# Seven joined parts in place of two fourth products in the first feed-forward stage of an encoder

## The chip, the core and the metric

The kernel runs on one core of a Trainium2 chip. A core has a matrix engine (TensorE, "PE" in the profile, with its weight loads on a row of their own, "PEld"), two engines for elementwise work (VectorE, "DVE", and ScalarE, "ACT"), GpSimd ("POOL"), which here issues the DMAs that add to what lies in the buffer, and SyncE ("SP"), which issues plain DMAs. All five run their own queues in order and wait for each other by semaphores. The metric is device time in microseconds (us) of one execution; lower is better.

## The reference

A two-layer encoder over 512 tokens of 1024 channels, float32. Each layer is a feed-forward stage (FFN), a mixer and a second FFN; so there are four FFNs, and the one that the change touches is the first of layer 0.

```python
D_MODEL, SEQ, DEPTH, D_FF = 1024, 512, 2, 2816
...
def swiglu(x, w_in, w_out):
    gu = x @ w_in
    g, u = jnp.split(gu, 2, axis=-1)
    return (jax.nn.silu(g) * u) @ w_out
...
for l in range(DEPTH):
    x = x + 0.5 * swiglu(rms_norm(x, ffn1_norm[l]), ffn1_w_in[l], ffn1_w_out[l])
    x = x + mixer(rms_norm(x, mix_norm[l]), ...)
    x = x + 0.5 * swiglu(rms_norm(x, ffn2_norm[l]), ffn2_w_in[l], ffn2_w_out[l])
return rms_norm(x, final_norm)
```

## The kernel before

**Precision.** Every float32 operand is split into a high part (rounded, type fp32r) and a low part (the rest). One product of two operands is three matmuls: high x high, low x high, high x low (`run`, L392 to L406).

**Weights.** They come from HBM in granules of 128 x 1024 (two contraction tiles of 128, 512 columns each), 512 KB apiece, into nine "raw" buffers (`ffn_raw`, L2024). For each granule ScalarE writes the high part `whi` (L205, L207) and VectorE the low part `wlo` (L212, L214); there are three buffers of each. The class `Stream` walks one list of items made in advance (`stage_items`), and the products take them in that order (`ws.next`). When an item's high part is made, the loads of the next eight items are issued (`fetch`, FETCH). An item may be a sum of two granules: either VectorE adds the second (`sum`, L200), or GpSimd issues a DMA that adds the second one into the first one's buffer (L166). `then` names a granule that is added by such a DMA after the low part has been made, so that the buffer serves a later item.

**Seven products for eight.** The up and gate projections are done by blocks of 512 columns of w_in. A block is a 2 x 2 matrix product (two halves of the contraction, gate and up columns; two halves of the tokens) and is computed by a Strassen-like scheme in seven products instead of eight. They are named 1 to 7 here, as in the code; each takes two granules and 24 matmuls of 128 x 512, and their results are joined on ScalarE and VectorE (`snap`, `less`, `gate`, `times`). There are five blocks, `jb` 0 to 4, after a first part of 256 + 256 columns that is done plainly into four banks `pcl` (L694 to L706). Block 0 is the *single block* (L984 to L1024); blocks 1 and 2, and 3 and 4, are *pairs* (`pair_block`, L899).

**Products joined over a pair.** The product 2 of both blocks of a pair has the same activations, and the weights of the two blocks stand for the two columns of another 2 x 2 product, this time within the contraction half. So the two products 2 are done together as seven inner products `b1` to `b7`, of one granule and 6 matmuls each (`inner`, L735), spread over the two blocks. In the three later FFNs the first pair's products 4 are done in the same manner, as `d1` to `d7`: `begin_deep` (L867) is a generator; its first step makes four sums of the activations on VectorE (`inner_parts`), splits them into `vh` and `vl` (`inner_split`) and does d1 into the bank rA; each further `next` does one more. Four are done in the single block (d1, d5, d6, d3), two in block 1 (d2, d7) and one in block 2 (d4). `kv` and `kw` keep their sums until the block adds them to `pa` (L957). In the first FFN the generator is an iterator over five numbers, so these steps do nothing, and products 4 are done in full in both blocks (L973).

**Items.** `INNER` (L37) says behind which product each inner part's item stands; the single block's items in the first FFN are 1, 2, 5, 6, 7, 3, 4 (ORDER_0), two granules each. Of a pair's parts, d1 takes one granule a, d5 the sum d of two granules (by a DMA), d6 d + a and d3 d + b (VectorE), d2 the granule b, d7 a sum c (by a DMA), d4 one granule. In the first FFN, b6 is d + a by VectorE; in the later ones b5's buffer gets a added by a DMA after b5, and b6 takes it as it is.

**The first FFN's single block.** Its work on VectorE and ScalarE is held in program order (`tc.manual_schedule`, L985) up to the roots of the row norms (`norm.roots`), since the input x arrives only then. `spread_root` (L767) then writes the 512 roots to HBM and reads them back spread over all partitions (`rd`, `rr`), on SyncE's queue, where the raw loads are issued too. `plain_out` (L773), which needs `rr`, comes in block 2 (L919). Elsewhere the engines' orders are the scheduler's, by program order and readiness.

Of the kernel before, what the change touches and what calls it, by code (L numbers as in the profile page):

```python
# [35 lines left out]
DEEP = 1  # L36
# [18 lines left out]
PAIRS = (1, 3)  # L55
# [49 lines left out]
def encoder_kernel(  # L105
# [120 lines left out]
    def stage_items():  # L226
        items, st = [], 0

        def add(*a, **k):
            items.append(Item(*a, stage=st, **k))  # L230

        made = {}

        def strassen(s, name, idx, sizes, order, dma=False):
            r = made.setdefault((s, name("a"), idx), {}) if dma and len(order) < 7 and order[0] > 2 else {}
            for q, q2 in () if r else (("a", ""), ("b", ""), ("c", "a"), ("d", "c")):
                r[q] = [
                    Raw((s, name(q), idx, g), n, *[(s, name(z), idx, g) for z in q2]) for g, n in enumerate(sizes)
                ]
            if dma and order is ORDER_W:  # L240
                keys = [[(s, name(z), idx, g) for z in "dca"] for g in range(len(sizes))]
                r["s"] = [Raw(z[0], n, *z[1:]) for z, n in zip(keys, sizes)]
            d2 = [Raw((s, name("d"), idx, g), n) for g, n in enumerate(sizes)]
            for m in order:
                yield m
                for g in range(len(sizes)):
                    a, b, c, d = [r[q][g] for q in "abcd"]
                    if m == 1:
                        add(a, neg=True)
                    elif m == 2:  # L250
                        add(b)
                    elif m == 3:
                        add(r["s"][g] if "s" in r else d, None if dma else b)
                    elif m == 4:
                        add(d2[g])
                    elif m == 5:
                        add(d, then=a.key if dma and order is not ORDER_W else None)
                    elif m == 6:
                        t = r["s"][g] if "s" in r else d
                        add(t, None if dma else a, then=b.key if dma else None)  # L260
                    else:
                        add(c)

        def four(*a):
            for _ in strassen(*a):
                pass

        def out_sizes(c):
            return (1024, 512) if c == 0 else (1024, 1024)

        def ffn(s):
            first = not items
            for g in range(4):
                add(Raw((s, "cl", g)), parts=2 if first and g < 2 else 1, pieces=2 if first and g == 0 else 1)
            parts = {}
            for j in range(NB):
                for q, to in (("b", j), ("d", j + 1)):
                    if to not in PAIRS or q == "d" and (to != DEEP or first):
                        continue
                    key = [[(s, q, to + z, g) for g in range(2)] for z in range(2)]  # L280
                    a, b, c = Raw(key[0][0]), Raw(key[0][1]), Raw(key[1][0], 1024, key[0][0])
                    d, d2 = Raw(key[1][1], 1024, key[1][0]), Raw(key[1][1])
                    of = {1: ((a,), True), 2: ((b,), False), 4: ((d2,), False), 7: ((c,), False)}
                    of.update({3: ((d, b), False), 6: ((d, a), False), 5: ((d,), False)})
                    parts.update({f"{q}{m}": (z, {"neg": neg}) for m, (z, neg) in of.items()})
                    if q == "b" and j == DEEP and not first:
                        parts["b5"] = (d,), {"then": a.key}
                        parts["b6"] = (d,), {}
                if not j:
                    order = ORDER_0 if first else ORDER_W  # L290
                else:
                    order = (1, 5, 6, 7, 3) if j in (DEEP, DEEP + 1) and not first else (1, 5, 6, 7, 3, 4)
                todo = []
                for m in strassen(s, lambda q: q, j, (1024, 1024), order):
                    for z in todo:
                        add(*parts[z][0], **parts[z][1])
                    todo = [z for z in INNER[j].get(m, "").split() if z in parts]
                for z in todo:
                    add(*parts[z][0], **parts[z][1])
            for order in ((1,), (2,), (5, 6, 7, 3), (4,)):  # L300
                for c in range(3):
                    four(s, lambda q: "o" + q, c, out_sizes(c), order)

        for l in range(L):
            ffn((l, 1))
            st += 1
            s = (l, 0)
            two = (1024, 1024)
            for g in VG:
                add(Raw((s, "v", g)), kept=g == VG[0])  # L310
            for g in range(3):
                add(Raw((s, "up", g), UC * len(UK[g]), (s, "uq", g)))
            for g in range(2):
                add(Raw((s, "un", g)), minus=(s, "um", g))
            for g in range(8):
                add(Raw((s, "qk", g)))
            for i in range(2):
                add(Raw((s, "fp", i), 1024, (s, "fq", i)))
                add(Raw((s, "fq", i)), minus=(s, "fp", i))
            for i in range(2):  # L320
                four(s, lambda q: "g" + q, i, two, ORDER_0[0 : 2 - i], True)
            for g in range(2):
                add(Raw((s, "n", 0, g)))
            for i, order in ((0, (5,)), (1, (2,)), (0, (6,)), (1, (5,)), (0, (7, 3)), (1, (6,)), (0, (4,)), (1, (7, 4, 3))):
                four(s, lambda q: "g" + q, i, two, order, True)
                st += not i and order[0] == 5
            for g in range(2):
                add(Raw((s, "n", 1, g)))
            four(s, lambda q: "w" + q, 0, two, ORDER_W, True)
            ffn((l, 2))  # L330
        return items
# [312 lines left out]
    def stage_ffn(norm, nxt, late):  # L644
# [217 lines left out]
        kept = {}  # L862
# [31 lines left out]
            S.activation(half(w, 0), ra, AF.Copy)  # L894
            yield

        deep = kept["d"] = iter(range(5)) if first else begin_deep()

        def pair_block(jb):  # L899

            f0 = 2 + 4 * jb
            one, deep = jb in PAIRS, jb in (DEEP, DEEP + 1) and not first
            pa = pair("A")
            product(pa, acts[1], K4, True)
            s1 = snap(pa)
# [71 lines left out]
        for jb in range(NB):  # L977
            f0 = 2 + 4 * jb
            if jb:
                if jb == 1:  # L980
                    inner_split("b", [z[1][:, :, 0:256] for z in (hx, lx)])
                pair_block(jb)
                continue
            if first and jb == 0:  # L984
                with tc.manual_schedule(engines={mybir.EngineType.DVE, mybir.EngineType.Activation}):  # L985
                    pa = pair("A")
                    product(pa, acts[1], K4, True)
                    for j in range(2):
                        t = snap(pcl[2 * j : 2 * j + 2])
                        pcl[2 * j : 2 * j + 2] = [t[:, 0, :], t[:, 1, :]]  # L990
                    s1 = snap(pa)
                    second(s1)
                    pb = pair("B")
                    product(pb, acts[5], K4, True)
                    sb = snap(pb)
                    norm.squares(1, 1)
                    product(pa, acts[6], K4, False, again=True, ahead=1)
                    s2 = snap(pa)
                    for _ in norm.roots(0, 4):
                        pass  # L1000
                spread_root()
            else:
                pa, pb, s1, sb = two(jb)
                settle_at()
                product(pa, acts[6], K4, False, again=True)
                s2 = snap(pa)
            settle_at()
            if not first:
                plain_out()
                next(deep)  # L1010
                second(s1)
            z1 = gate(s1, 0)
            product(pa, acts[7], K4, False, again=True)
            less(pa, sb)
            next(deep)
            product(pb, acts[3], K4, False, again=True)
            less(pb, s2)
            z2 = gate(s2, 1)
            times(z2, [sb[:, 0, :], sb[:, 1, :]], 1)
            next(deep)  # L1020
            product(pa, acts[4], K4, False, again=True)
            times(z1, pa, 0)
            next(deep)
            late_at += [(z2, 1, f0, 4), (z1, 0, f0, 4)]  # L1024
# [1220 lines left out]
```

## Time and profile before

| | |
|---|---|
| Median of 3 runs | 1855.47 us (1854.03 to 1858.47) |
| Profiled execution, its own time | 1854.71 us |
| Its span, first to last instruction | 1852.8 us |
| Granted TensorE clock, mean | 0.999 |
| HBM read, written | 411.83 MB, 6.30 MB |
| DMA rate over the span | 227 GB/s |

The profile has one execution. Busy time is given per engine; a matmul is pipelined, so the start of the next one tells more than its own duration. In the tables of stretches each row is a window in us from the span's start, with each engine's busy time and, in brackets, its instructions, then the granted clock, the DMA engines' mean busy share and GB/s. In the groups a row has line, engine, operation, tiles, shapes and count, then busy us and mean ns of one, then the idle time of the engine just before them and what ended it. In the timelines a row has start, duration, engine, line, operation and tiles; in square brackets the idle time before it and what ended that. "SPq" is an issue by SyncE's queue.

### The profile page before, as it was taken

The numbers are of one execution on the slowest core, as the hardware profiler recorded it, in microseconds if no ns is written. First come the engines' busy times: TensorE is split into PE (matmuls) and PEld (weight loads), VectorE is DVE, ScalarE is ACT, GpSimd is POOL, SyncE is SP. The second block draws the span as 40 slices with busy tenths as digits, with TensorE's granted clock in tenths as the row PEclk, the third lists the DMA queues.
The fourth block names the chain that finished last, engine by engine and source line by source line (L and its number), as shares of the span: only waits on it lengthen the run. The fifth ranks groups of instructions, "written<-read, shape, count | busy, mean of one in ns | idle before, by whom it ended". The sixth has DMA issues, their size and how long they took to land.

```text
span 1852.8 us, 26162 instructions
## 1 busy us (share of the span) xinstructions
PE 1842.4 (99%) x9514; PEld 1567.5 (85%) x9514; DVE 1592.3 (86%) x1979; ACT 1213.9 (66%) x1795; POOL 204.1 (11%) x244
## 2 busy tenths in 40 slices
PE   9999999999999999999999999999999999999998
PEld 7888888889998888888888888888899988888876
DVE  8888899758879889889979988996687798998988
ACT  6666665758656666666666666667676576666665
POOL 0011010100211011101001110101002100110010
PEclk9999999999999999999999999999999999999999
DMA  9888788874998599869769986978749974998695
GB/s 300 239 243 234 217 239 257 264 189 135 248 256 220 127 257 268 238 200 267 236 138 261 270 228 205 261 239 260 202 142 255 235 222 131 262 262 241 194 275 177
DMA packets 122801, 421.29 MB, mean 227 GB/s; under 512 B 15776, under 2 KB 15904, under 8 KB 122672
## 3 DMA queue, kind: packets, MB, share of 16 engines
q1 hardware_dynamic: 88832, 300.41, 46.4%
q0 software_dynamic: 33408, 118.43, 33.9%
q8 instruction: 74, 1.21, 0.3%
q10 hardware_dynamic: 432, 0.79, 0.1%
q14 instruction: 55, 0.45, 0.1%
HBM read 411.83 MB, written 6.30 MB: 226 GB/s over the span
## 4 chain that ended last, share of the span: by engine, by line
PE 96%; DVE 2%; DMA 2%; issue 0%; ACT 0%; POOL 0%; ACTq 0%; DVEq 0%; POOLq 0%
PE A L403 9%; PE A L406 9%; PE A L404 9%; PE o L406 7%; PE o L403 7%; PE o L404 7%; PE B L403 5%; PE B L406 5%; PE B L404 5%; PE cl L689 4%; PE ps L403 3%; PE ps L404 3%; PE ps L406 3%; PE tr L660 2%; DMA raw<-in_wst_dram 2%; PE tr L488 1%
## 5 line engine op out<-in xcount | busy, mean ns | idle before, releaser
L214 DVE TENSOR_TENSOR wlo<-raw,whi 128x1024 fp32r<-128x1024 f32 (+1 forms) x546 | 644.7, 1192 | 143.2 <-ACT whi L207 140.7
L207 ACT ACTIVATE whi<-raw 128x1024 fp32r<-128x1024 f32 (+1 forms) x546 | 559.6, 1033 | 309.2 <-PE A L404 74.8
L166 POOL DMA_DIRECT2D raw<-in_wst_dram x192 | 166.1, 871 | 1431.6 <-DMA raw<-in_wst_dram 614.5
L200 DVE TENSOR_TENSOR raw<-raw,raw 128x1024 f32<-128x1024 f32 (+1 forms) x147 | 175.1, 1194 | 2.5 <-DMA raw<-in_wst_dram 0.2
L205 ACT ACTIVATE whi<-raw 128x1024 fp32r<-128x1024 f32 (+1 forms) x87 | 90.5, 1040 | 72.0 <-issue 26.0
L212 DVE SCALAR_TENSOR_TENSOR wlo<-raw,whi 128x1024 fp32r<-128x1024 f32 (+1 forms) x87 | 103.7, 1197 | 6.0 <-ACT whi L205 5.9
L403 PE MATMUL A<-whi,xh 128*128 128x512 f32 x272 | 105.8, 389 | 0.0
L404 PE MATMUL A<-whi,xl 128*128 128x512 f32 x272 | 105.8, 389 | 0.0
L637 ACT ACTIVATE sn<-A 128x512 f32<-128x512 f32 x96 | 56.1, 590 | 45.7 <-PE A L406 45.7
L406 PE MATMUL A<-wlo,xh 128*128 128x512 f32 x272 | 78.3, 389 | 0.0
L795 ACT ACTIVATE th<-sn,r 128x512 f32<-128x512 f32 x80 | 55.3, 713 | 25.9 <-DVE sn L642 22.1
L403 PE MATMUL B<-whi,t1h 128*128 128x512 f32 x160 | 62.7, 392 | 0.0
L403 PE MATMUL A<-whi,t2h 128*128 128x512 f32 x160 | 62.5, 391 | 0.0
L403 PE MATMUL A<-whi,t3h 128*128 128x512 f32 x160 | 62.4, 390 | 0.0
L404 PE MATMUL A<-whi,t2l 128*128 128x512 f32 x160 | 62.3, 389 | 0.0
L404 PE MATMUL B<-whi,t1l 128*128 128x512 f32 x160 | 62.3, 389 | 0.0
L404 PE MATMUL A<-whi,t3l 128*128 128x512 f32 x160 | 62.3, 389 | 0.0
L403 PE MATMUL B<-whi,xh 128*128 128x512 f32 x160 | 62.2, 389 | 0.0
L404 PE MATMUL B<-whi,xl 128*128 128x512 f32 x160 | 62.2, 389 | 0.0
L404 PEld LDWEIGHTS A<-whi,xl 128*128 128x128 f32 x272 | 51.1, 188 | 10.6
L406 PEld LDWEIGHTS A<-wlo,xh 128*128 128x128 f32 x272 | 51.1, 188 | 10.6
L403 PEld LDWEIGHTS A<-whi,xh 128*128 128x128 f32 x272 | 51.0, 188 | 10.6
(539 smaller groups left out, 4986.2 us busy)
## 6 DMA issues: line engine op xcount, KB each, us to landing
raw<-in_wst_dram SPq DMA_DIRECT2D x506, 512.0 KB
raw<-in_wst_dram POOLq DMA_DIRECT2D x209, 512.0 KB, 8.4
raw<-in_wst_dram SPq DMA_DIRECT2D x28, 256.0 KB
vc<-vd SPq DMA_DIRECT2D x28, 256.0 KB
bm<-in_near_dram SPq DMA_DIRECT2D x16, 384.0 KB
vd<-v SPq DMA_DIRECT2D x8, 512.0 KB
dft<-in_dft_dram POOLq DMA_DIRECT2D x4, 514.0 KB, 9.8
x<-in_xin_dram SPq DMA_DIRECT2D x4, 512.0 KB
```

The source lines that it names most:

```text
L166: z = G.dma_start(out=self.t, in_=wst[GRAN_AT[plus]][:, 0 : self.n], accum_op=ALU.add)
L200: V.tensor_tensor(self.raw.t, self.raw.t, self.add.t, ALU.add)
L205: S.activation(self.out[0][:, cs], self.raw.t[:, cs], AF.Copy, scale=-1.0)
L207: S.activation(self.out[0][:, cs], self.raw.t[:, cs], AF.Copy)
L212: self.last = V.scalar_tensor_tensor(lo, t, -1.0, hi.bitcast(F32), ALU.mult, ALU.subtract)
L214: self.last = V.tensor_tensor(lo, t, hi.bitcast(F32), ALU.subtract)
L403: PE.matmul(ps, lh, rh, start=start, stop=False, skip_group_check=again)
L404: PE.matmul(ps, *((lh, rl) if w == "l" else (ll, rh)), start=False, stop=False, skip_group_check=again)
L406: PE.matmul(ps, *((ll, rh) if w == "l" else (lh, rl)), start=False, stop=stop, skip_group_check=again)
L637: S.activation(t[:, b, :], ps[b], AF.Copy)
L689: PE.matmul(pcl[cb], lh[:, cs[cb]], rh, start=first and n == 0 and len(order) == 3, stop=last and n == len(order) - 1,)
L795: S.activation(th[:, b, :], g[:, b, :], AF.Silu, scale=norm.r[:, c : c + 1])
```

## The change

The first FFN too gets the seven parts d1 to d7 for its first pair, blocks 1 and 2, and no longer does products 4 of these blocks. As in the other FFNs, d1, d5, d6 and d3 stand in the single block, where the first step now comes after product 6 and before product 7. b5's buffer gets a by a DMA and b6's sum on VectorE goes. In block 2 the transposes of the block before (`settle_at`) move from before product 5 to after b7, as in the other FFNs. The other three FFNs and the mixers are as before.

```diff
@@ stage_items, ffn
-                    if to not in PAIRS or q == "d" and (to != DEEP or first):
+                    if to not in PAIRS or q == "d" and to != DEEP:
                         continue
...
-                    if q == "b" and j == DEEP and not first:
+                    if q == "b" and j == DEEP:
                         parts["b5"] = (d,), {"then": a.key}
                         parts["b6"] = (d,), {}
...
-                    order = (1, 5, 6, 7, 3) if j in (DEEP, DEEP + 1) and not first else (1, 5, 6, 7, 3, 4)
+                    order = (1, 5, 6, 7, 3) if j in (DEEP, DEEP + 1) else (1, 5, 6, 7, 3, 4)
@@ stage_ffn
-        deep = kept["d"] = iter(range(5)) if first else begin_deep()
+        deep = kept["d"] = begin_deep()
...
-            one, deep = jb in PAIRS, jb in (DEEP, DEEP + 1) and not first
+            one, deep = jb in PAIRS, jb in (DEEP, DEEP + 1)
...
             settle_at()
             if not first:
                 plain_out()
-                next(deep)
+            next(deep)
+            if not first:
                 second(s1)
             z1 = gate(s1, 0)
```

## The prediction

> **What bounds the kernel now.** I read the page first, then the table of stretches, then the timeline of each engine around the first FFN's single block. The page:
>
> ```profile
> span 1852.8 us, 26162 instructions
> ...
> PE 1842.4 (99%) x9514; PEld 1567.5 (85%) x9514; DVE 1592.3 (86%) x1979; ACT 1213.9 (66%) x1795; POOL 204.1 (11%) x244
> ...
> PE 96%; DVE 2%; DMA 2%; issue 0%; ACT 0%; POOL 0%; ACTq 0%; DVEq 0%; POOLq 0%
> ```
>
> TensorE is busy 99% of the span, and the chain of waits runs through it for 96%. A change therefore pays by the matmuls that it saves, and costs by each time that TensorE is made to wait. The table of stretches has one row per FFN, each from the first matmul of the single block's first product to the first matmul of the down projection:
>
> ```profile
> 28.66:223.76 195.10, 195.10 (x894) 162.06 (x893) 164.89 (x185) 125.13 (x166) 20.71 (x24) 1.00 0.83 231
> 623.14:817.28 194.14, 193.91 (x887) 160.99 (x886) 168.81 (x181) 126.33 (x161) 19.90 (x23) 1.00 0.80 226
> 949.12:1142.99 193.87, 193.87 (x887) 160.99 (x886) 169.09 (x181) 126.78 (x161) 19.90 (x23) 1.00 0.81 228
> 1542.31:1736.25 193.94, 193.94 (x888) 160.99 (x886) 169.21 (x181) 126.64 (x161) 19.89 (x23) 1.00 0.80 226
> ```
>
> Columns: stretch, length, then busy time of TensorE, its weight loads, VectorE, ScalarE and GpSimd, then clock, DMA share, GB/s. The first row is the FFN that the change touches; the other three already compute the fourth products in seven parts. They are 0.96, 1.23 and 1.16 us shorter. That is the size of the prize, with the parts' own waits in it.
>
> **The change part by part. TensorE.** The price of a matmul, from the timeline of TensorE:
>
> ```profile
> 28.66 0.39 PE L403 MATMUL A<-whi,xh 128*128 128x512 f32 x1
> 34.10 0.39 PE L403 MATMUL C<-whi,xh 128*128 128x512 f32 x1
> 49.96 0.61 PE L406 MATMUL A<-wlo,t2h 128*128 128x512 f32 x2
> 50.58 0.50 PE L403 MATMUL A<-whi,t3h 128*128 128x512 f32 x1
> 50.91 0.39 PE L404 MATMUL A<-whi,t3l 128*128 128x512 f32 x1
> 223.76 0.39 PE L403 MATMUL o<-whi,c1h 128*128 128x512 f32 x1
> ```
>
> A full product is 24 matmuls (4 contraction tiles x 2 blocks x 3 terms) and takes 34.10 - 28.66 = 5.44 us, so 0.2267 us each. Two fourth products go: 48 matmuls, -10.88 us. Seven parts come, each one granule of 6 matmuls: 42, +9.52 us. Net -1.36 us.
>
> Between products 6 and 7 the matmul after 49.96's pair was due at 49.96 + 2 x 0.2267 = 50.41 and started at 50.58, and the one behind it 0.33 us later instead of 0.23: 0.27 us of waiting. ScalarE shows why; product 7 writes over the banks that these two copies read:
>
> ```profile
> 49.93 0.59 ACT L637 ACTIVATE sn<-A 128x512 f32<-128x512 f32 x1
> 51.36 0.60 ACT L637 ACTIVATE sn<-A 128x512 f32<-128x512 f32 x1
> ```
>
> The first ends at 50.52. Part d1 (1.36 us, own bank rA) now stands between the two products and covers it: -0.27 us, if d1 itself is ready. In the later FFNs the sum 195.10 - 0.27 - 1.36 = 193.47 was missed by 0.67, 0.40 and 0.47 us; I take +0.5 for such waits of the order (0.4 to 0.7).
>
> **VectorE.** Durations, from the groups of the first FFN's single block and, for the two forms that it lacks, of the second FFN:
>
> ```profile
> L214 DVE TENSOR_TENSOR wlo<-raw,whi 128x1024 fp32r<-128x1024 f32 x12 | 14.6, 1221 | 2.0 <-ACT whi L207 1.9
> L200 DVE TENSOR_TENSOR raw<-raw,raw 128x1024 f32<-128x1024 f32 x4 | 4.8, 1221 | 0.0
> L411 DVE TENSOR_TENSOR vl<-v,vh 128x1024 fp32r<-128x1024 f32 x1 | 1.2, 1219 | 0.0
> L716 DVE TENSOR_TENSOR v<-xr 128x256 f32<-128x256 f32 x1 | 0.4, 418 | 0.0
> ...
> L957 DVE TENSOR_TENSOR kv<-A,kv 128x512 f32<-128x512 f32 x2 | 1.4, 682 | 0.0
> L884 DVE TENSOR_TENSOR kv<-rB,kv 128x512 f32<-128x512 f32 x1 | 0.7, 687 | 0.0
> ```
>
> Added: seven low parts for four (3 x 1.22), the sums of d6 and d3 for b6's, which becomes a DMA (1 x 1.22), four part sums (4 x 0.42), one vl (1.22), three subtractions and four additions out of PSUM (7 x 0.68): 3.66 + 1.22 + 1.68 + 1.22 + 4.76 = 12.5 us over 195 us. Where it falls matters more than the sum:
>
> ```profile
> 28.66:67.09 38.43, 38.43 (x170) 31.38 (x168) 33.51 (x48) 26.77 (x40) 6.02 (x7) 1.00 0.79 204
> 67.09:108.30 41.21, 41.21 (x192) 34.36 (x191) 35.56 (x36) 25.62 (x33) 4.32 (x5) 1.00 0.95 260
> ...
> 623.14:666.93 43.79, 43.79 (x194) 35.96 (x192) 39.28 (x46) 30.63 (x37) 3.46 (x4) 1.00 0.55 153
> ```
>
> The first row is the first FFN's single block, the last the second FFN's, with its parts. Into the first come d1, d5, d6, d3: four lows 4.88, two sums 2.44, part sums 1.68, vl 1.22, one subtraction 0.68 = 10.9 us, against 4 x 1.36 = 5.44 us of matmuls. VectorE would need 33.5 + 10.9 = 44.4 us in 38.43 + 5.44 - 0.27 = 43.6 us; the second FFN's needs 39.28 of 43.79. The shortage hides only behind what VectorE does early:
>
> ```profile
> 35.34 1.22 DVE L757 TENSOR_TENSOR xr<-xr,xr 128x1024 f32<-128x1024 f32 x1
> ...
> 44.69 2.52 DVE L214 TENSOR_TENSOR wlo<-raw,whi 128x1024 fp32r<-128x1024 f32 x2
> 47.13 2.35 DVE L200 TENSOR_TENSOR raw<-raw,raw 128x1024 f32<-128x1024 f32 x2
> 51.81 1.22 DVE L214 TENSOR_TENSOR wlo<-raw,whi 128x1024 fp32r<-128x1024 f32 x1
> ```
>
> At 47.13 it already makes the sums for product 3, whose matmuls start at about 50.58 + 5.44 = 56.0: these 2.35 us can be put off. Chain to d1 from the end of product 6's lows at 47.2: d1's low, the four part sums (0.34 each, the 0.42 overlapping a little), vh on ScalarE (1.06, as the high of that size in the last rows of the next part), vl: 47.2 + 1.22 + 1.36 + 1.06 + 1.22 = 52.06. TensorE wants vl at 50.41 + 0.23 = 50.64. Wait 1.4 us. Lower bound 0 (the part sums' input, L757, is ready at 36.56, so they can fill a hole of VectorE before), upper bound 1.4 + 2.35 = 3.75 (the sums of product 3 stay in front). I take 1.4, by the order of the code, in which the part sums stand behind product 6. ScalarE's own extra in the block (vh and four highs at 1.06, three copies out of PSUM at 0.59: 7.1 us) I cost at nothing; its cover is the 38.43 - 26.77 = 11.7 us that it is idle there now, and without that it would add up to 7.1 - 5.44 = 1.7 us.
>
> **DMA and the queues.** Five loads come (d1's, d5's, d3's, d7's, d4's tiles), four go, and three more accumulations (d5's, d7's, and one behind b5) stand in GpSimd's queue. SyncE's loads are in order behind the row scales' round trip through HBM:
>
> ```profile
> 41.37 14.63 SPq L164 DMA_DIRECT2D raw<-in_wst_dram  x8
> 56.61 0.39 SPq L770 DMA_DIRECT2D rd<-r  x1
> ...
> 69.92 0.33 SPq L771 DMA_DIRECT2D rr<-rd  x1
> 70.34 3.49 SPq L164 DMA_DIRECT2D raw<-in_wst_dram  x2
> ...
> 56.81 0.86 POOL L166 DMA_DIRECT2D raw<-in_wst_dram  x1 [23.42 <-DVE r L427]
> 60.22 0.86 POOL L166 DMA_DIRECT2D raw<-in_wst_dram  x1 [0.37 <-issue]
> DMA to landing us min/median/max: 13.0/14.7/16.5
> DMA to landing us min/median/max: 7.5/7.8/8.0
> 73.84 1.06 ACT L207 ACTIVATE whi<-raw 128x1024 fp32r<-128x1024 f32 x1 [1.87 <-DMA raw<-in_wst_dram]
> 75.66 0.39 PE L403 MATMUL B<-whi,t1h 128*128 128x512 f32 x1
> ```
>
> From 58.7 to 70.3 no load is issued but waits for the store of the roots to land; the three accumulations issued from 56.81 to 60.22 took 13.0 to 16.5 us, the two after 70 took 7.5 and 8.0 (the two landing rows, in this order). They are block 1's product 5 and b5. By the order of the code they are raw tiles 18 to 20 now; with d1, d5 and d3 before them they become 21 to 23. Nine buffers exist; thirteen tiles are out before 41.37 and eight more by 56, so 21, for twelve given back. With d1's and d5's tiles held longer I count 19 or 20. So product 5's tiles now miss the boat: load from 70.34, second in line at 3.16 us (3.49 less one issue), landing about 2 us later (0.5 MB at 260 GB/s), accumulation 7.8, high 1.06: 70.34 + 3.16 + 2 + 7.8 + 1.06 = 84.4. TensorE wants it at 75.66 + 4 x 1.36 + 1.36 (d2) - 0.27 + 1.4 = 83.6. Late by 0.8, and the accumulations behind it, one after another, perhaps by more. Bounds: 0 (the tiles go out before the store, as now) and 0.8 + 14.7 - 7.8 = 7.7 (the slow accumulation). I take 1.5, nearer the quick landing, since the store is over by then.
>
> **Sum.** -1.36 - 0.27 + 0.5 + 1.4 + 1.5 = +1.77 us. The profiled execution took 1854.71 us (1.9 around its span of 1852.8); 1854.71 + 1.77 = 1856.5. The median of the runs shown is 0.76 above that execution, so 1857.2. What a measurement can tell from no change is 0.2%, 3.7 us either side of 1855.47, so 1851.8 to 1859.2: the forecast is no measurable difference, a shade slower. Its own range is 1855.0 to 1859.5.
>
> **Rivals.** *Clean gain*: both new waits come out at their lower bounds and the first FFN becomes like the later ones: -1.1 us, 1854.4. For it: three rows above, same code. Against it: 44.4 us of VectorE work in 43.6 us, and the round trip, which the later FFNs do not have inside the block (their DMA share there is 0.55, here 0.79). *Loads miss the boat, slow landing*, the other side: if the accumulations for product 5 land as slowly as the three now do, late by the midpoint of 0.8 and 7.7, 4.25 us, in place of 1.5: 1857.2 + 2.75 = 1860.0. It decides from the point at which tile 21 is issued after 69.92. *VectorE becomes the bound*: it can never run at 100%, since each low waits for its high:
>
> ```profile
> L214 DVE TENSOR_TENSOR wlo<-raw,whi 128x1024 fp32r<-128x1024 f32 x40 | 48.4, 1223 | 10.9 <-ACT whi L207 10.9
> ```
>
> This is the second FFN's first three blocks (623.14 to 738.95, so 9.4% idle for highs). If the first FFN's need a third of that idle share, 1.4 us in the single block, the shortage there is 44.4 + 1.4 - 43.6 = 2.2, and as much again in block 1 (35.56 + two lows 2.44 + two subtractions and two additions 2.72 - two lows 2.44 - b6's sum 1.22 = 37.1 of 41.21 - 5.44 + 2.72 = 38.5, before 9.4% of idle time and what the single block left over): 4.4 in place of the 1.4 of d1, 1860.2. [...] Against it: the second FFN's VectorE is 90% busy in its single block (39.28 of 43.79), and TensorE is idle for 0.23 us in that whole stretch.
>
> **How the numbers follow.** Forecast 0.42, clean gain 0.20, slow landing 0.20, VectorE bound 0.13, others 0.05. Slower by over 0.2%: most of the two slow rivals (0.26) and the upper end of the forecast (0.11): 0.37. Faster by over 0.2% would need 3.7 us where the matmuls save 1.36 and the waits 0.27: 0.03. Same: 0.60. The range takes in the clean gain less half a microsecond and most of the slow cases: 1853.8 to 1862.5.
>
> **What would show it.** The first FFN's stretch (195.10) becomes 195.10 + 1.8 = 196.9; at 194.0 the clean gain is right, at 199 or more a slow rival. The wait before product 7 is gone; rA's first matmul follows product 6 by up to 1.4 us, waiting for vl. In block 1, TensorE waits at B<-whi,t1 for a high, which waits for a DMA. If TensorE waits in the single block beyond d1 for lows, it is VectorE. The forecast is wrong if the later FFNs or the mixers, which the change leaves alone, shift by more than half a microsecond.

## The result, and the profile after

The changed kernel took 1860.51 us (median of 20 runs, 1858.50 to 1862.89) against 1855.39 us for the kernel before (20 runs beside them, 1854.03 to 1859.90): a ratio of 1.0025, 95% interval 1.0018 to 1.0031. That is slower by some 5 us, or 0.25%: a little over the 0.2% that the prediction took as the bound of what can be told from no change, with that bound inside the interval. The profiled execution took 1861.19 us. Its page, and its table of stretches (the columns as before: the first three FFNs, from the first product to the down projection):

```profile
span 1859.4 us, 26182 instructions
...
PE 1844.1 (99%) x9508; PEld 1568.2 (84%) x9508; DVE 1601.6 (86%) x1995; ACT 1217.6 (65%) x1803; POOL 206.7 (11%) x247
```

```profile
28.59:230.22 201.63, 197.31 (x887) 161.57 (x886) 174.65 (x201) 129.98 (x174) 23.23 (x27) 0.99 0.85 233
629.53:824.16 194.63, 193.90 (x888) 161.14 (x886) 168.96 (x181) 126.43 (x161) 19.89 (x23) 1.00 0.81 225
956.00:1150.87 194.87, 193.92 (x887) 161.14 (x886) 169.07 (x181) 126.42 (x161) 19.93 (x23) 1.00 0.82 227
```

The loss is in the first row: 195.10 became 201.63, 6.53 us longer. The two rows below moved by 0.49 and 1.00 us, but such shifts come without the change: a control run told of below (e7) shows 195.65 and 196.19 there. TensorE's waits in the first FFN's single block and block 1 (engine, line, what it waited for: us in total, times, longest):

```profile
PE rA L403 <- ACT whi L207: 1.8, 1, 1.8
PE A L403 <- ACT whi L207: 0.7, 1, 0.7
PE A L403 <- ACT whi L205: 0.7, 1, 0.7
PE qB L403 <- ACT whi L207: 0.6, 1, 0.6
PE A L406 <- DVE wlo L214: 0.4, 1, 0.4
```

The second, third and fifth are in the single block, counted up to block 1's first matmul (at 74.97), the first and fourth in block 1. The single block first, on TensorE's timeline:

```profile
49.90 0.62 PE L406 MATMUL A<-wlo,t2h 128*128 128x512 f32 x2
50.35 0.39 PE L403 MATMUL rA<-whi,xh 128*128 128x512 f32 x1
...
62.14 0.61 PE L406 MATMUL B<-wlo,xh 128*128 128x512 f32 x2
63.45 0.50 PE L403 MATMUL A<-whi,xh 128*128 128x512 f32 x1 [0.70 <-ACT whi L207]
...
65.19 0.40 PE L404 MATMUL A<-whi,xl 128*128 128x512 f32 x1
65.99 1.19 PE L406 MATMUL A<-wlo,xh 128*128 128x512 f32 x4 [0.40 <-DVE wlo L214]
...
68.40 0.40 PE L403 MATMUL rB<-whi,vh 128*128 128x512 f32 x1
...
73.70 0.61 PE L406 MATMUL rB<-wlo,xh 128*128 128x512 f32 x2
74.97 0.50 PE L403 MATMUL A<-whi,xh 128*128 128x512 f32 x1 [0.65 <-ACT whi L205]
```

Part d1 (50.35) follows product 6 without a gap, so the old wait before product 7 is gone. Its operands are `xh` and `xl`, not `vh` and `vl`. With 0.2267 us for a matmul, the first of 63.45 was due at 62.14 + 0.45 = 62.59 and came 0.86 late; those of 65.99 and 74.97 came 0.57 and 0.82 late. With some matmuls behind them that start another 0.1 us late, the single block loses 2.8 us. d5 (into rB) does not stand behind product 7, where the code has it, but at 68.40, in the middle of product 4. VectorE and ScalarE tell why:

```profile
60.76 0.16 DVE L427 SCALAR_TENSOR_TENSOR r<-rt,r 128x4 f32<-128x4 f32 x1
...
63.71 0.42 DVE L716 TENSOR_TENSOR v<-xr 128x256 f32<-128x256 f32 x1
...
68.42 1.22 DVE L411 TENSOR_TENSOR vl<-v,vh 128x1024 fp32r<-128x1024 f32 x1
```

```profile
62.34 1.06 ACT L207 ACTIVATE whi<-raw 128x1024 fp32r<-128x1024 f32 x1 [2.11 <-PE B L404]
...
70.72 1.06 ACT L207 ACTIVATE whi<-raw 128x1024 fp32r<-128x1024 f32 x1 [0.97 <-PE rB L404]
```

The part sums run only at 63.71, behind the last step of the roots (60.76), and `vl` is begun at 68.42. The weights of d5 are split but cannot be used, so they occupy one of the three high buffers, and those of d6, three items later, a second one: the high part at 70.72 waits for a matmul of d5 into rB to give its buffer back. Block 1, on TensorE and on ScalarE, and the granted clock there:

```profile
91.26 0.50 PE L403 MATMUL qB<-whi,vh 128*128 128x512 f32 x1 [0.63 <-ACT whi L207]
...
92.52 0.73 PE L406 MATMUL qB<-wlo,vh 128*128 128x512 f32 x2
95.09 0.69 PE L403 MATMUL rA<-whi,vh 128*128 128x512 f32 x1 [1.84 <-ACT whi L207]
...
98.56 0.43 PE L403 MATMUL A<-whi,t2h 128*128 128x512 f32 x1
```

```profile
90.15 1.06 ACT L207 ACTIVATE whi<-raw 128x1024 fp32r<-128x1024 f32 x1 [5.42 <-DMA raw<-in_wst_dram]
93.98 1.06 ACT L207 ACTIVATE whi<-raw 128x1024 fp32r<-128x1024 f32 x1 [2.78 <-DMA raw<-in_wst_dram]
```

```profile
95.00:99.00 4.00, 3.91 (x10) 3.10 (x11) 3.69 (x4) 4.00 (x7) 0.00 (x0) 0.57 1.05 241
```

b5 (into qB) and d7 (into rA) wait for highs, and these for DMA. b5's first matmul was due at 90.47 and came 0.79 late; with a wait of 0.23 for its low part (at 92.52) and the later start of the second matmul behind each (0.33 us instead of 0.23), b5 costs 1.2. d7's first was due at 92.52 + 0.33 + 0.23 = 93.08 and came at 95.09, 2.0 us late. Then the eight steps from 95.09 to 98.56 take 3.47 us instead of 8 x 0.2267 = 1.81, at a clock of 0.57: 1.7 us more. So block 1 loses 4.9 us. Together: 195.10 - 1.36 (matmuls) - 0.27 (the old wait) + 2.8 + 4.9 = 201.2; the rest to 201.63, some 0.5, is shorter stalls, none over 0.21 us.

Where the late tiles come from, by GpSimd's accumulations and by DMA rates (last column, GB/s), after and before:

```profile
62.80 0.87 POOL L166 DMA_DIRECT2D raw<-in_wst_dram  x1 [16.61 <-DMA raw<-in_wst_dram]
65.45 0.86 POOL L166 DMA_DIRECT2D raw<-in_wst_dram  x1 [1.78 <-DMA raw<-in_wst_dram]
81.01 0.86 POOL L166 DMA_DIRECT2D raw<-in_wst_dram  x1 [14.70 <-DMA raw<-in_wst_dram]
82.28 0.87 POOL L166 DMA_DIRECT2D raw<-in_wst_dram  x1 [0.40 <-issue]
...
DMA to landing us min/median/max: 13.1/13.4/13.7
DMA to landing us min/median/max: 9.0/10.3/11.6
```

```profile
64.00:68.00 4.00, 3.60 (x15) 2.35 (x14) 3.59 (x7) 1.98 (x3) 0.86 (x1) 1.00 0.28 29
68.00:72.00 4.00, 4.00 (x19) 3.11 (x18) 2.49 (x4) 3.02 (x6) 0.00 (x0) 1.00 0.36 32
```

```profile
64.00:68.00 4.00, 4.00 (x20) 3.30 (x19) 4.00 (x6) 2.78 (x3) 0.00 (x0) 1.00 0.44 108
68.00:72.00 4.00, 4.00 (x19) 3.34 (x18) 2.77 (x3) 1.66 (x2) 0.00 (x0) 1.00 1.08 229
```

Product 5's accumulations are out at 62.80 and 65.45 (the first landing row, 13.1 to 13.7 us) and in time. The next two, of b5 and d7, go out at 81.01 and 82.28 and land after 9.0 and 11.6 us, at 90.04 and 93.88, just where the highs of 90.15 and 93.98 wait. Between 64 and 72 us the DMA engines move some 30 GB/s; before, three accumulations had been issued by then, after, two. SyncE's queue has issued the store of the roots and waits for it (`rd`, 512 pieces of 4 bytes); the loads of b5, d7 and one more tile leave behind the read:

```profile
60.95 0.39 SPq L770 DMA_DIRECT2D rd<-r  x1
71.19 0.34 SPq L771 DMA_DIRECT2D rr<-rd  x1
71.62 1.98 SPq L164 DMA_DIRECT2D raw<-in_wst_dram  x3
```

From 60.95 to 71.62 no load is issued, and from 65 on little more than the two accumulations is under way, so the low rate does not by itself show slow DMA engines. Runs e2 and e5 do.

### The profile page after: what moved, and what is told of

Same layout as the page of the kernel before. It is cut to its first block, busy times and chain, and to the rows that moved or that the text cites. A ratio compares the mean times of both kernels' runs of the same rounds, so it can differ in the third digit from the quotient of the medians.

```text
span 1859.4 us, 26182 instructions
## 1 busy us (share of the span) xinstructions
PE 1844.1 (99%) x9508; PEld 1568.2 (84%) x9508; DVE 1601.6 (86%) x1995; ACT 1217.6 (65%) x1803; POOL 206.7 (11%) x247
## 4 chain that ended last, share of the span: by engine, by line
PE 89%; DMA 6%; DVE 3%; issue 1%; ACT 1%; POOL 0%; ACTq 0%; SPq 0%; DVEq 0%; POOLq 0%
PE A L404 8%; PE A L403 8%; PE A L406 8%; PE o L406 6%; PE o L404 6%; PE o L403 6%; DMA raw<-in_wst_dram 5%; PE B L404 4%; PE B L403 4%; PE B L406 4%; PE cl L689 4%; PE ps L403 3%; PE ps L404 3%; PE ps L406 3%; PE tr L660 2%; DVE wlo L214 1%
## 5 line engine op out<-in xcount | busy, mean ns | idle before, releaser
L214 DVE TENSOR_TENSOR wlo<-raw,whi 128x1024 fp32r<-128x1024 f32 (+2 forms) x548 | 646.6, 1191 | 144.2 <-ACT whi L207 142.8
L207 ACT ACTIVATE whi<-raw 128x1024 fp32r<-128x1024 f32 (+2 forms) x548 | 561.5, 1033 | 317.0 <-PE A L404 73.1
L205 ACT ACTIVATE whi<-raw 128x1024 fp32r<-128x1024 f32 (+1 forms) x88 | 91.5, 1041 | 76.2 <-PE B L404 27.2
L403 PE MATMUL A<-whi,xh 128*128 128x512 f32 x256 | 100.1, 391 | 1.4 <-ACT whi L207 0.7
L404 PE MATMUL A<-whi,xl 128*128 128x512 f32 x256 | 99.8, 390 | 0.0
L406 PE MATMUL A<-wlo,xh 128*128 128x512 f32 x256 | 73.9, 390 | 0.4 <-DVE wlo L214 0.4
```

What stands on the lines that cost most here:

```text
L205: S.activation(self.out[0][:, cs], self.raw.t[:, cs], AF.Copy, scale=-1.0)
L207: S.activation(self.out[0][:, cs], self.raw.t[:, cs], AF.Copy)
L214: self.last = V.tensor_tensor(lo, t, hi.bitcast(F32), ALU.subtract)
L403: PE.matmul(ps, lh, rh, start=start, stop=False, skip_group_check=again)
L404: PE.matmul(ps, *((lh, rl) if w == "l" else (ll, rh)), start=False, stop=False, skip_group_check=again)
L406: PE.matmul(ps, *((ll, rh) if w == "l" else (lh, rl)), start=False, stop=stop, skip_group_check=again)
```

## The experiments

Three causes were held against each other: the **late part sums** (single block), the **blocked queue** (the read of the roots waits in SyncE's queue, and the raw loads behind it), and the **small-piece store** (while it lasts, the DMA engines are slow for everybody). Each time stands beside the kernel before on the same chip, 1855.2 to 1856.2 us.

**e1: the part sums early.** `begin_deep` gets a first step of its own, called ahead of the roots:

```diff
             inner_split("d", t4)
+            if first:
+                yield
...
                     s2 = snap(pa)
+                    next(deep)
                     for _ in norm.roots(0, 4):
```

> The changed kernel with d's part sums and their split (vh, vl) made right after product 6, ahead of the chain of the roots, in place of behind it; nothing else moves. Theory V (VectorE makes the sums too late, so d5 and d6 wait for vl and hold two of the three whi/wlo buffers, and product 4 goes on one): d5 follows product 7 again, the waits of the matrix engine from 62 to 75 us (2.8 us in the changed kernel) fall under 0.7, the first FFN's stretch from 201.6 to about 199. Theory L (the loads of b5's and d7's tiles stand behind the round trip of the row scales): the waits before b5 and d7 and the slow matmuls after them (4.9 us) stay within 1.5 us of that. If VectorE is simply short of time, the 2.8 us only move to another place of the single block and the stretch stays at 201 or more.

Measured: 1862.25 us (ratio 1.0029, 1.0018 to 1.0040), stretch 202.04. d5 is back at its place (57.2 us), but 1.67 us of waits stay in product 4 and before block 1's first matmul, and the store, now behind more loads, is issued at 69.58 and holds the read for 14.3 us. TensorE then waits 3.2 and 1.6 us in product 7 of block 1. One cause treated, and the other got dearer.

**e2: the read moved out of the single block**, to the start of block 2, so that SyncE's loads pass it; the store stays:

```diff
-            spread["r"] = t = slot(F32, "rr", (2, T))[:, 0, :]
...
+            spread["d"] = rd
+            if norm.idx:
+                spread_back()
...
+            if first and jb == 2:
+                spread_back()
```

> The changed kernel with the read of the spread roots (rr) issued at the start of block 2, where it is needed next, in place of right behind its store; SyncE's loads no longer stand behind it. Theory L: the waits before b5 and d7 go, with the slow matmuls after them; the stretch falls from 201.6 to about 196.7, the time by some 5 us. Theory V: the 2.8 us of the single block stay. Rival to L (the DMA engines are full or the adding DMAs are slow in themselves): b5 and d7 still wait, together 2 us or more, and the time changes by less than 2 us.

Measured: 1859.42 us (1.0019, 1.0010 to 1.0028), stretch 201.06. Its waits on TensorE in the single block and block 1, the DMA rates, and the part sums:

```profile
PE qB L403 <- ACT whi L207: 4.0, 1, 4.0
```

```profile
68.00:72.00 4.00, 4.00 (x20) 3.30 (x19) 4.00 (x5) 3.48 (x4) 0.00 (x0) 1.00 0.54 35
```

```profile
50.49 0.42 DVE L716 TENSOR_TENSOR v<-xr 128x256 f32<-128x256 f32 x1
```

Two things are to be seen. Nothing blocks SyncE's queue, and b5's load leaves at 66.41 (71.62 in the changed kernel), yet the rate is as low and b5 waits 4.0 us: the blocked queue alone is not the cause, and theory L missed. And with the read gone from this place the scheduler's order has the part sums at 50.49, among the steps of the roots, and the single block loses 0.35 us instead of 2.8, against theory V. So the read costs the single block its order, without anything there needing its data.

**e3: control, the same edit in the kernel before.**

> Control: the kernel before with the same later read of the roots. Its matrix engine waits 0.3 us in the whole stretch, so by theory L nothing is to be gained: stretch 195.1 within 0.5, time unchanged within 0.1%.

Measured: 1856.10 us (1.0000, 0.9991 to 1.0009), stretch 195.51.

**e4: e1 and e2 together.**

> The changed kernel with both edits. If L and V are two separate causes, both go: stretch about 194 as in the later FFNs (194.1, 193.9, 193.9), time 1 us under the kernel before. If one cause hides another, the stretch stays over 196.

Measured: 1860.41 us (1.0021, 1.0012 to 1.0030), stretch 199.60. The single block loses 0.1 us; d7 waits 2.2 us in block 1 (2.1 in the view of waits), the granted clock is 0.89 from 88 to 92 us and 0.68 from 92 to 96, product 7 of block 1 loses 0.7 and a transpose in block 2 1.0. The first cause is gone, the second stays.

**e5: no store and no read.** The roots are spread in block 1 by four transposes on TensorE and VectorE's products with the identity:

```diff
+        def spread_pe():
...
+            for c in range(TB):
+                z = slice(c * P, (c + 1) * P)
+                V.tensor_scalar(w[:, 1, z], ident, 0.0, norm.r[:, c : c + 1], ALU.mult, ALU.add)
+                PE.transpose(tr[:, z], w[:, 1, z], ident)
+            S.activation(w[:, 0, :], tr, AF.Copy)
...
-                spread_root()
```

> The changed kernel with the first FFN's roots spread over the partitions by four transposes on the matrix engine in block 1, without the store to HBM and the read back. Theory S (the store of 512 roots of 4 bytes keeps the DMA engines from moving weights for some 10 us, so the tiles of b5 and d7 land late): no stretch of 4 us between 56 and 80 us with under 60 GB/s, no wait before b5 and d7 over 0.3 us, no slow matmuls; the first FFN's stretch falls from 201.6 to 197 or less, the time by 4 to 5 us. Theory B (nine raw buffers are too few with d's tiles held longer, loads go out when buffers come free): the waits before b5 and d7 stay at 2 us or more, the stretch over 199. The 2.8 us of the single block (62 to 75 us) stay by both.

Measured: 1855.12 us (0.9996, 0.9987 to 1.0004). Its stretch, and the DMA rates:

```profile
28.59:224.22 195.63, 194.69 (x891) 161.26 (x890) 174.72 (x205) 130.76 (x175) 22.81 (x27) 1.00 0.86 239
...
68.00:72.00 4.00, 4.00 (x19) 3.34 (x18) 4.00 (x5) 3.56 (x5) 0.86 (x1) 1.00 0.93 215
```

No gap in the rates (202, 215 and 281 GB/s in the three windows from 64 to 76 us), no wait at b5 or d7, clock 1.00. Against e2, 5.4 us of the stretch are gone, though the transposes come on top. On every engine the other instructions stand in the same order in both, so apart from the spread's own this pair differs by the store and the read alone. b5's load leaves SyncE at 66.41 in e2 and at 66.92 in e5, and its accumulation, which needs the loaded tile, at 82.02 and at 73.51: beside the store the load takes 9 us longer, with no queue blocked. The 2.8 us of the single block, which were to stay, became 0.8.

**e6: e5 with the part sums early; e7: the spread by TensorE in the kernel before.**

> As the run without the store, and d's part sums ahead of the roots. By S and V together (late part sums cost the single block 2.8 us): stretch 194 to 195, time 0.5 to 1.5 us under the kernel before. By B: the stretch stays over 197.

> Control: the kernel before without the store. Its matrix engine hardly waits in this stretch (0.3 us), so by S and by B nothing is gained: stretch 195.1 to 195.9 (four transposes more), time within 0.1%.

Measured: e6 1855.60 us (0.9996, 0.9987 to 1.0005), stretch 195.30, single block 0.1 us of waits, 0.8 at the transposes of its own. e7 1855.77 us (0.9995, 0.9986 to 1.0004), stretch 195.58. The early sums are worth little where the read does not disturb the order (0.7 us of the single block), and the spread by TensorE is worth nothing to the kernel before. Nor does the change pay once both losses are gone: e6's stretch, 195.30, is no shorter than 195.10. Of the 1.6 us that the change saves, the spread takes 1.2 back: the wait of 0.8, and some 0.1 us for each of the four transposes (an estimate: the sixteen at 80.55 in the changed kernel took 1.66). The rest goes to short waits.

**e8 and e10: the store in 16-byte pieces**, 128 instead of 512, the same kernel twice; `plain_out` reads `rr` with a stride to match:

```diff
-            nc.sync.dma_start(out=bass.AP(tensor=rd.tensor, offset=rd.offset, ap=[[1, P], [P, TB]]), in_=norm.r)
+            to = [[1, P], [P, TB]] if norm.idx else [[TB, P], [1, TB]]
+            nc.sync.dma_start(out=bass.AP(tensor=rd.tensor, offset=rd.offset, ap=to), in_=norm.r)
...
```

> The changed kernel with the roots stored as 128 pieces of 16 bytes in place of 512 of 4, and read by plain_out with a stride. If the store's cost goes by its pieces, it lands in a quarter of the 10.2 us (2 to 4 us) and the waits before b5 and d7 shrink by more than half; if it does not, it lands after 8 us or more and they stay.

> The changed kernel with the roots stored as 128 pieces of 16 bytes, once more and timed. Small-piece store theory with the late part sums left in: stretch 196.5 to 197.5, time 1.0 to 2.0 us above the kernel before, and 3 to 4.5 us below the changed kernel. If the first look at it was luck: waits at b5 and d7 are back and the stretch is above 199.

Measured: e8 1857.09 us (one run), stretch 197.02; e10 1856.36 us (1.0007, 0.9998 to 1.0016), as expected. Of e10 the stretch, the rates, SyncE's wait for the store (9.8 us in the changed kernel, by the same view), and the landing times of the accumulations issued between 60 and 70 us:

```profile
28.57:225.85 197.28, 195.12 (x887) 160.47 (x886) 175.95 (x201) 130.51 (x174) 23.44 (x27) 1.00 0.87 238
...
64.00:68.00 4.00, 3.23 (x13) 2.08 (x12) 3.59 (x8) 1.40 (x2) 1.03 (x2) 1.00 0.48 88
68.00:72.00 4.00, 4.00 (x18) 3.09 (x18) 2.89 (x3) 3.00 (x5) 0.00 (x0) 1.00 1.06 273
```

```profile
SPq L772 <- DMA rd<-r: 3.9, 1, 3.9
```

```profile
DMA to landing us min/median/max: 7.4/8.4/9.5
```

On every engine the instructions stand in the same order as in the changed kernel (part sums at 64.30, 3.4 us lost in the single block); only the pieces are larger and lie in another order. The store is waited for 3.9 us, the accumulations land in 7.4 and 9.5 us instead of 13.1 and 13.7, and block 1's waits with the lowered clock are gone (1.00 from 84 to 104 us): 201.63 - 197.28 = 4.4 us. That is the price of the small-piece store. It is paid in two ways, and this pair changes both: the store holds the read and the loads behind it in SyncE's queue (b5's load leaves at 66.55 instead of 71.62, its accumulation at 75.79 instead of 81.01), and what is under way beside it is slow. In the changed kernel the queue is what makes b5's load late (from its issue to the accumulation it is 9.4 us there and 9.2 in e10); e2 against e5 shows that the slow transfers suffice without it.

**e9: 16-byte store and early part sums.**

> The changed kernel with two edits at once: the roots stored as 128 pieces of 16 bytes, and the part sums of the activations with their split put ahead of the row norms' roots. If the two losses are the small-piece store (about 4.9 us in block 1) and the late part sums (about 2.8 us in the single block), both are gone: first FFN's stretch 193.5 to 194.5 us (201.63 in the changed kernel, 195.10 before), no wait of TensorE over 0.4 us at b5 or d7 and under 0.5 us in sum in the single block, and a time 0.7 to 1.6 us below the kernel before. Rival: with the part sums early VectorE is merely late elsewhere (as with the part sums alone, where 1.67 us stayed in the single block); then the stretch is 195.2 to 196.2 and the time within 1 us of the kernel before.

Measured: 1858.90 us (1.0019, 1.0010 to 1.0027), stretch 200.42: both theories missed. TensorE's two longest waits in the stretch, and SyncE's:

```profile
PE tr L660 <- ACT at L664: 2.6, 1, 2.6
PE A L403 <- ACT sn L637: 1.1, 1, 1.1
```

```profile
SPq L772 <- DMA rd<-r: 9.2, 1, 9.2
```

b5 and d7 do not wait, as expected. But 1.4 us stay in the single block, much as in e1, which the rival had foretold; and the wait for the store is 9.2 us again. It is issued at 69.25, behind loads just issued, and while the read waits for it only one load leaves SyncE's queue in ten microseconds. TensorE then waits 1.3 us in product 7 of block 1 and 2.8 us at the transposes of block 2, both times for ScalarE, which had waited for tiles shortly before (2.5 us at 99.34, 2.3 us at 125.42). This points to the blocked queue, which here can cost something even without small pieces; no run tells it apart from the late issue of the store. In block 2 ScalarE also waits 0.49 us (at 131.03) for a product with `rr`, which takes 1.07 us here (see e11). The three remedies together (large pieces, early sums, read moved) were not tried.

**e11: the 16-byte store in the kernel before; e12: the kernel before with the 4-byte store issued twice.**

> Control: the kernel before with the roots stored as 128 pieces of 16 bytes. In the kernel before nothing waits for the tiles that the store delays, so the shorter store is worth nothing there: stretch 194.9 to 195.6, time within 0.7 us of the kernel before; the wait of the read for the store falls to about 4 us. If the store costs the kernel before as well, the stretch falls below 194.5.

> The kernel before, with the roots stored a second time in 512 pieces of 4 bytes, right behind the first store and ahead of the read; no other edit. Small-piece store theory: the stretch of low DMA rate (under 40 GB/s) grows from some 10 us to some 20, and tiles in flight land late, so that TensorE now waits for highs in block 1 here too: stretch over 197. Rival (the added loads and accumulations of the change are what makes tiles late, the store only happens to lie beside them): the stretch stays within 0.7 us of 195.1.

Measured: e11 1856.69 us (1.0002, 0.9993 to 1.0011), stretch 196.16, outside the expected range; the read waits 5.2 us for the store; the rate between 64 and 68 us is 242 GB/s in place of 108, so the gap goes here too, and is worth nothing. What the stretch has over 195.10 is one wait of 0.9 us for a low part in block 2; `rr` is now read with a stride, and each of VectorE's four products with it takes 1.07 to 1.10 us instead of 0.68. e12 1855.85 us (one run), stretch 195.08, with this rate:

```profile
64.00:68.00 4.00, 4.00 (x19) 3.30 (x19) 4.00 (x6) 2.70 (x3) 0.00 (x0) 1.00 0.46 46
```

A miss: the second store does not double the gap (46 GB/s against 108 between 64 and 68 us, and 217 against 229 in the four after that), and the time stays. The second store leaves at 56.97, 0.44 us behind the first, and the read waits 8.9 us for the first (11.2 in the kernel before): the price of such a store is therefore not so much per piece here. What it consists of stays open. The result is the one that the rival of e12 foretold, that the added loads and accumulations make the tiles late; but e5, e6 and e10 have the same added loads and accumulations, and b5 and d7 do not wait there. The kernel before has the same store and a gap of its own (98 and 108 GB/s from 60 to 68 us), but no tile that is waited for falls into it.

## Why the prediction was right and wrong

**The direction and the range.** The forecast was "no measurable difference, a shade slower", with a range of its own of 1855.0 to 1859.5. The sign held; 1860.51 lies above that range and above the 1859.2 that it took for the end of "no difference". Only the wide range, 1853.8 to 1862.5, which takes in the slow rivals, has it. The likeliest case was 3.3 us too low, and two of its terms were right in sign for reasons that the runs do not bear out, so that the wide range held is in part luck.

**Matmuls (-1.36) and the wait before product 7 (-0.27)**: as predicted; with them the sum of the terms comes out at the measured stretch. **Waits of the order (+0.5)**: 0.5.

**d1 waits for vl (+1.4)**: wrong at its first step. d1 multiplies a slice of the split activations themselves and did not wait; d5 is the first that needs `vh` and `vl`. The prediction had the part sums stand behind product 6 by the order of the code; they ran at 63.71, 13 us later than in e2. Price 2.8 us, paid before product 4, within it and behind it through the buffers that d5 and d6 hold. The upper bound of that term, 3.75, covers the size but not the mechanism. With the read in its place the single block loses 2.8 us (the changed kernel), 3.4 (e10), 1.7 (e1) and 1.4 (e9, sums early like e1); with the read moved or gone 0.35 (e2), 0.8 (e5) and 0.1 (e4, e6). In e10 the store is short (waited for 3.9 us), so it is not the wait for it that costs, but the order that the scheduler makes with the read in this place. Why it makes that order is not shown.

**Product 5's tiles miss the boat (+1.5)**: the step that failed is the count. The prediction put 19 or 20 raw tiles ahead of the round trip; 22 were out (the 22nd at 60.28), as many as before, and product 5's are 21 and 22. The next ones, b5's and d7's, went out behind it. For these the mechanism of the term held, a load behind the read, but its prices did not: the landing of the load, put at about 2 us, took 9.4 us up to the accumulation (71.62 to 81.01), and the accumulations took 9.0 and 11.6 in place of 7.8. Nor is the blocked queue the only way to such a loss: e2 shows the tiles late with the queue open. Measured 4.9 us, of which 1.7 are a lowered clock that the sum did not have at all.

**ScalarE's own extra (at nothing)** was not quite nothing. The last 0.9 of the 2.8 us came behind a ScalarE that was busy without a break from 70.72: d3's high, late for d5's buffer, then two copies of the parts' results out of PSUM (0.58 and 0.59) and gate steps, and only then the high that TensorE waited for.

**The rivals.** *Clean gain* fell by 6 us. *Slow landing*, 1860.0, came nearest to 1860.5 by its number, and accumulations did land slowly; but its condition (tile 21 issued after 69.92) was not met: tile 21 had been loaded by 62.80, when its accumulation left. That its number fits is luck. *VectorE the bound* fell: e6 has the same joined parts and VectorE at 174.38 of 195.30 us in that stretch, and loses 0.1 us in the single block. VectorE's order, not its load, cost time there.

**What would show it**: TensorE does wait in block 1 for a high that waits for a DMA, but at b5 and d7, not at product 5. The single block does wait for lows beyond d1 (0.4 us), though VectorE's load is not the cause. And a later FFN did shift by more than half a microsecond (1.00), which was to show the forecast wrong; e7 has such shifts without the change.

## What to carry to other kernels

A gap in the DMA rate that costs nothing today can be a price held in reserve, as it was here (before, 98 and 108 GB/s from 60 to 68 us and no tile waited for inside it; after, 29 and 32 GB/s from 64 to 72 us and 4.9 us lost in block 1): before loads are added, look in the table of rates for the gap and count which tiles would have to be issued inside it. Check which operand each moved product reads in the timeline, not by the name of the group that it belongs to. And treat a round trip through memory as the three costs that it had here: what its store slows (35 GB/s from 68 to 72 us in e2, 215 without it in e5), what its read blocks in the queue (no load from 60.95 to 71.62), and what the scheduler does to the order of the work around it (2.8 us of the single block, 0.35 with the read moved in e2); removing one can raise another (e1, e9), so try them apart.

## What the hardware showed

A store of 2 KB in 512 pieces of 4 bytes was waited for 9.8 us in the changed kernel, and other transfers were slow beside it: in e2, with loads issued at 66.41, 68.80 and 70.64, the DMA engines moved 35 GB/s from 68 to 72 us, against 215 in e5 without the store; and an accumulation issued at 65.17 landed after 13.2 us in e2, the two issued at 65.61 and 68.01 in e5 after 5.6 to 8.1. In 128 pieces of 16 bytes at the same place it was waited for 3.9 us (e10); in the kernel before, 11.2 us became 5.2 (e11). Behind loads just issued, the 16-byte store too was waited for 9.2 us (e9). The store in pieces larger than 16 bytes was not run.

TensorE's granted clock was 0.57 over the 4 us after d7's wait (95 to 99 us), behind waits of 0.8 and 2.0 us with 1.8 us of work between them. In e4, with one wait of 2.2 us at d7, it was 0.89 from 88 to 92 us and 0.68 from 92 to 96. In e9 a wait of 2.8 us lowered nothing:

```profile
130.00:133.00 3.00, 0.54 (x3) 0.10 (x1) 3.00 (x4) 2.51 (x6) 0.00 (x0) 1.00 1.00 299
133.00:136.00 3.00, 2.86 (x15) 2.46 (x16) 3.00 (x6) 1.76 (x5) 0.00 (x0) 1.00 0.36 146
```

So the wait of 2.0 us on TensorE cost 3.7 in the changed kernel, with the 1.7 of the lowered clock, and the longer one in e9, at a clock of 1.00, only itself. What decides whether the clock falls is not shown by these runs.
